# Forget-gate attention: probabilities in fewer SBUF slots, value products of two query tiles in one round, gated outputs fetched a round before their split

## The chip, the cores and the metric

The kernel is one program on one core of a Trainium2 chip. The metric is the device time of one execution in microseconds. A profiled execution gives, beside its time, the span from the first to the last instruction and a record of every engine. PE is the matrix engine (TensorE), PEld its weight loads, ACT is ScalarE, DVE is VectorE, POOL is GpSimd, and SP is SyncE, which issues most of the DMA transfers. The granted clock is the share of full speed at which PE was allowed to run.

## The reference, cut to what matters

The program is a stack of three blocks (latent attention with a sliding window, forget-gate attention, then an mLSTM mixer, cross attention and a mixture of experts). The change lies in the second, `fox_layer`, with 1024 tokens, 16 heads of width 64, and query blocks of 128:

```python
def causal_block_attention(q, k, v, log_cum=None):
    ...
        s = jnp.einsum('bqhd,bkhd->bhqk', qi, k, preferred_element_type=jnp.float32) * scale
        if lc_t is not None:
            ci = lax.dynamic_slice_in_dim(lc_t, start, QBLOCK, axis=2)
            s = s + ci[..., :, None] - lc_t[..., None, :]
        ...
        s = jnp.where(mask, s, -jnp.inf)
        p = jax.nn.softmax(s, axis=-1)
        return jnp.einsum('bhqk,bkhd->bqhd', p.astype(v.dtype), v)

def fox_layer(x, g_in, w_in, b_f, w_out):
    ...
    o = causal_block_attention(...)
    return x + (o.reshape(B, S, FOX_WIDTH) * jax.nn.silu(gate)) @ w_out
```

## The kernel before, in words

The function `fox` works through 64 steps n = 8p + i: p is one of 8 pairs of heads (a = 0 and 1 are the two heads of a pair), i is one of 8 query tiles of 128 rows. Each step goes through four stages.

- `score(n)`: PE multiplies queries and keys, three products of split numbers for each head; each head uses 64 of the 128 rows of the array. Rows of keys reach up to the query tile, so the width is 128(i+1). The results lie in PSUM banks `ps` (three) and `pd` (two). Then POOL adds the mask to the forget terms (`dm`), and DVE adds the forget terms and takes the row maximum into the tile `P` (L1259).
- `soft(n)`: ACT takes the exponential in place and sums it (L1267), DVE takes the reciprocal (`rinv`), POOL multiplies `P` by it (L1270).
- `turn(n)`: PE transposes `P` block by block into PSUM banks `pt` (two, up to four blocks in each), and ACT copies each bank into the tile `PT` (L1286). The copies of steps n = 2z and n = 2z + 1 lie side by side in one `PT`, 256 columns wide.
- `outs(n)`: PE multiplies the values by `PT` (L1301), with 64 columns of the array for each head, into the bank `po`. Of the pair z, the even step does the first half of the key blocks and the odd step the second half. Every order row of this product is two records in the trace. After i = 3 and i = 7, DVE multiplies by the gate (`go`, L1309) and ACT issues the DMA that stores `go` in the DRAM tensor `god`.

The rounds t = -2 to 65 are written out in one loop: `outs(t-2)`, `score(t+2)`, then `turn(t+1)` woven with fill work, then `soft(t+2)`. The fill is the projection of queries, keys and gates of the next pair of heads (and, for some, of values), L342 to L344, for t below 54: eight pieces for each pair of heads, six in the last. From t = 54 to 57 there is no fill. From t = 58 (p = 7) the fill is the key and value projection of the later cross attention (L1895, input `s<-x_wkv`, output `kvo`, stored in `kvd`), with as many units in each round as `FOX_FILL` says, and `ahead(t-56)`, which prepares the output projection of this layer by the table `FOX_AHEAD`: ('w', j) fetches and splits j pieces of `o_wo`, ('g', j) loads the pieces j of `god` (two halves of the tokens) into `gor` and splits each into `fh` (ACT, L348) and `fl` (DVE, L349). Then `out_proj` multiplies them (L342 to L344 again).

Order: on PE and SP the written order of the loop stands. ACT, DVE and POOL are ordered by a scheduler when the program is built; once built, every engine runs its list from the top to the bottom, so an instruction that waits holds all that stand behind it on its engine. SP's list is one queue of DMA issues: a load that waits for room holds the loads behind it.

Memory: `k.slot` gives one of 41 slots of 128 x 1024 numbers; `P`, `PT`, `V`, `x_wkv` and the split pieces live there. `k.xslot` gives one of three buffers; in this stage they hold the forget terms `lcb` of two heads (L1181, two DMAs for each pair of heads) and `gor`.

Of the kernel before, what the change touches and what calls it, by code (L numbers as in the profile page):

```python
# [58 lines left out]
LAM = 0  # L59
OUT_TILES = 4  # L60
FOX_FILL = {58: 1, 59: 2, 60: 1, 61: 2, 62: 1, 63: 1}
FOX_AHEAD = {2: (('w', 1),), 3: (('w', 1),), 4: (('g', 0),), 5: (('g', 1),), 6: (('w', 2), ('g', 2)), 7: (('w', 2),), 8: (('w', 2),), 11: (('g', 3),)}
MLA_W = (4, 0, 0.5, 1, 31)
MLA_U = 0
SW_AT = (1, 2, 3)
# [402 lines left out]
def weave(gens):  # L468
    gens = [g for g in gens if g is not None]
    while gens:  # L470
        for g in list(gens):
            try:
                next(g)
            except StopIteration:
                gens.remove(g)
# [639 lines left out]
def fox(k, ft, resid, after_tile):  # L1115
    nc, A = k.nc, k.A
# [6 lines left out]
    for i in range(NT):  # L1123
        ps = k.psd()
        for kt in range(8):
            wt, j = wv[kt // 3], kt % 3
# [15 lines left out]
    for b in range(2):  # L1142
        ps = k.pst()
        for t in range(4):
            i = b * 4 + t
            nc.tensor.matmul(ps[:16, t * 128:(t + 1) * 128], ab[:, i * 16:(i + 1) * 16], k.triu, start=True, stop=True)
        for t in range(4):
            i = b * 4 + t
            dst = nlc[:, i * 128:(i + 1) * 128]
# [9 lines left out]
    god = k.dram([8, 128, 1024], "god")  # L1159
    P, PT, po, M, WV = {}, {}, {}, {}, {}  # L1160
# [69 lines left out]
    def val(p, a, j):  # L1230
        c = p % 2 * 128 + a * 64
        return V[p // 2][j // 4][:, j % 4, c:c + 64]

    def score(n):

        p, i = divmod(n, 8)
        w = (i + 1) * 128
        qh, ql, kh, kl = qk[p]
        ps = {}
        for c in range(0, w, 512):  # L1240
            m = min(512, w - c)
            for a in range(2):
                ps[c, a] = k.psd() if c and a else k.pss()
            for l, r in ((qh, kh), (qh, kl), (ql, kh)):
                for a in range(2):
                    h = slice(a * 64, a * 64 + 64)
                    nc.tensor.matmul(ps[c, a][:, :m], l[h, i * 128:w], r[h, c:c + m], start=l is qh and r is kh, stop=l is ql)  # L1247
        for a in range(2):
            P[n, a] = k.slot([128, 1024], name="P")
            dm = k.small([128, 128], "dm", bufs=3)  # L1250
            nc.gpsimd.tensor_add(dm, lcb[p][a][:, i * 128:w], k.mask)  # L1251
            M[n, a] = 1e30
            for c in range(0, w, 512):
                m = min(512, w - c)
                for c0, c1, b in ((c, min(c + m, w - 128), lcb[p][a]), (w - 128, c + m, dm)):
                    if c1 <= c0:
                        continue
                    mx = k.small([128, 1], "m", bufs=12)
                    nc.vector.tensor_tensor_reduce(P[n, a][:, c0:c1], ps[c, a][:, c0 - c:c1 - c], b if b is dm else b[:, c0:c1],  # L1259
                                                   -1.0, M[n, a], OP.add, OP.min, mx)  # L1260
                    M[n, a] = mx

    def soft(n):
        w = (n % 8 + 1) * 128
        for a in range(2):
# [3 lines left out]
            nc.vector.reciprocal(ri, sm)  # L1269
            nc.gpsimd.tensor_scalar(sb[:, :w], sb[:, :w], ri, 0.0, op0=OP.mult, op1=OP.add)  # L1270

    def turn(n):
        i, z = n % 8, n // 2
        for a in range(2):
            p = P.pop((n, a))
            for c in range(0, i + 1, 4):
                m, q = min(4, i + 1 - c), (z, a, c // 4)
                if q not in PT:
                    PT[q] = k.slot([128, 4, 256], name="PT")
                pt = k.pst()  # L1280
                for j in range(m):
                    st["T"] = nc.tensor.transpose(pt[:, j * 128:(j + 1) * 128], p[:, (c + j) * 128:(c + j + 1) * 128], k.ident)  # L1282
                dst = PT[q][:, :m, n % 2 * 128:(n % 2 + 1) * 128]
                src = pt[:, :m * 128].rearrange("p (j n) -> p j n", j=m)
                if (a + c // 4) % 4 < 3:
                    nc.scalar.copy(dst, src)  # L1286
                else:
                    nc.vector.tensor_copy(dst, src)
                yield

    def outs(n):
        p, i = divmod(n, 8)
        if i % 4 == 0:
            po[0] = k.pso()
        o, half = po[0], i // 2 + 1
        last = half * 2 - 1
        for j in range(i % 2 * half, (i % 2 + 1) * half):
            n0 = 128 if j == last else 0
            cols = slice((last - 1) % 4 * 128 + n0, (last % 4 + 1) * 128)
            for a in range(2):  # L1300
                nc.tensor.matmul(o[a * 64:(a + 1) * 64, cols], val(p, a, j), PT[n // 2, a, j // 4][:, j % 4, n0:],  # L1301
                                 start=j == 0, stop=j == last)
            if j % 4 == 3 or j == last:
                for a in range(2):
                    PT.pop((n // 2, a, j // 4))
        if i % 4 == 3:
            t = k.slot([128, 512], name="go")
            cols = slice(i // 4 * 512, (i // 4 + 1) * 512)
            nc.vector.scalar_tensor_tensor(t, o, 0.5, gt[p][:, cols], op0=OP.mult, op1=OP.mult)  # L1309
            k.q.dma_start(out=god[p, :, cols], in_=t)  # L1310
# [5 lines left out]
    def fill(t):  # L1316

        p, i = divmod(t, 8)
        if t < 0:
            return [units[-1][t + 6]()]  # L1320
        if p >= 7:
            return k.mem.fill(FOX_FILL, t) + [ahead(t - 56)]
        if i == 0:
            u, g = prep(p + 1), p // 2 + 1
            if p < 6:
                u += [L(v_unit, g, x + p % 2 * 2) for x in range(2)]
                if p % 2 == 0:
                    u[2], u[4] = L(v_weights, u[2], g, 0), L(v_weights, u[4], g, 1)
            units[p] = u
        return [units[p][i]()] if i < len(units[p]) else []  # L1330

    go, W = FT(k), []

    def ahead(i):

        yield
        for what, j in FOX_AHEAD.get(i, ()):
            if what == "w":
                for _ in range(j):
                    W.append(k.w_get(k.fo[len(W)], 0))  # L1340
                    yield
            else:
                for hf in range(2):
                    t = k.xslot([128, 2, 512], name="gor")
                    nc.sync.dma_start(out=t, in_=god[2 * j:2 * j + 2, :, hf * 512:(hf + 1) * 512].rearrange("k p n -> p k n"))
                    hi, lo = go.piece(hf, j)
                    k.split(hi, lo, t)
                    yield

    a, b, c = FOX_SKEW  # L1350
    with k.tc.manual_schedule(engines=FOX_MAN):
        for t in range(-a, 64 - c):
            if 0 <= t + c:
                outs(t + c)
            if t + a < 64:
                score(t + a)
            weave(([turn(t + b)] if 0 <= t + b < 64 else []) + (fill(t) if t < 64 else [ahead(t - 56)]))
            if t + a < 64:
                soft(t + a)
# [788 lines left out]
class Moe:  # L2148
# [212 lines left out]
    def place(self, part, i0, row, col, iota, lo, hi, acc, t, B, ch, ps):  # L2361


        k, V, TT, w = self.k, self.k.nc.vector, self.k.nc.vector.tensor_tensor, hi - lo
        per = lambda v, n: v.unsqueeze(2).to_broadcast([128, 4, n])
        if part == 0:
            gg = self.gates[:, i0 * 2:i0 * 2 + 4]
            ident = t[:, 1016:1020]
            tok = self.tok[:, i0:i0 + 2].unsqueeze(2).to_broadcast([128, 2, 2])
            TT(ident.rearrange("p (n j) -> p n j", j=2), tok, row.rearrange("p (n j) -> p n j", j=2), op=OP.subtract)  # L2370
            rh = B["rh"] = k.slot([128, 4, 128], name="rh")
            ch = B["ch"] = ch().rearrange("p (n a w) -> p n a w", n=4, a=2)
            TT(rh, self.iota.unsqueeze(1).to_broadcast([128, 4, 128]), per(row, 128), op=OP.is_equal)
            TT(ch[:, :, 0, :], iota[:, lo:hi].unsqueeze(1).to_broadcast([128, 4, w]), per(col, w), op=OP.is_equal)
            V.tensor_mul(ch[:, :, 1, :], ch[:, :, 0, :], per(gg, w))
            V.tensor_mul(ch[:, :, 0, :], ch[:, :, 0, :], per(ident, w))
        elif part == 1:
            B["pl"] = ps()
            for n in range(4):
                k.nc.tensor.matmul(B["pl"][:, 0:2 * w], B["rh"][:, n, :], B["ch"][:, n, :, :].rearrange("p a b -> p (a b)"),  # L2380
                                   start=n == 0, stop=n == 3)
        else:
            acc = acc.rearrange("p (a b) -> p a b", a=2)[:, :, lo:hi]
            V.tensor_add(acc, acc, B["pl"][:, 0:2 * w].rearrange("p (a b) -> p a b", a=2))
            B.clear()
# [546 lines left out]
```

## Time and profile before

| what | us |
|---|---|
| median of 3 runs | 2276.36 (2274.25 to 2277.02) |
| the profiled execution | 2273.73 |
| its span | 2272.0 |
| PE busy in the span | 2177.8 |

The profiled execution is 2.63 us below the median, and 1.73 us of it lie outside the span. The rows that the prediction uses stand further down. In rows of a timeline, the first number is the start, the second how long the record or the merged records lasted, xN how many were merged; a bracket at the end tells how long the engine sat idle before it, and what released it. Records of matmuls overlap (they are pipelined), so the pace is read from the start of one to the start of the next.

### The profile page before, as it was taken

What the parts mean: (1) busy time and instruction counts of PE and PEld (TensorE: products, weight loads), DVE (VectorE), ACT (ScalarE), POOL (GpSimd) and SP (SyncE); (2) the same over time, 40 slices, a digit from 0 to 9 for tenths busy, and PEclk for the clock granted to TensorE, in tenths of its full rate; (3) what the DMA queues carried; (4) which work ended last, traced back from release to release, by engine and by line L of the source; (5) the groups of instructions that cost most, each with busy time, mean ns of one, the idle gap of its engine ahead of it and who ended that gap; (6) DMA issues with size and microseconds to landing.
All of it is one profiled execution on the core that took longest, in us unless ns stands there. A gap on an engine that the chain in (4) does not pass through costs nothing. (4 is left out here: it accounts for less than half of the span.)

```text
span 2272.0 us, 33492 instructions
## 1 busy us (share of the span) xinstructions
PE 2177.8 (96%) x12596; PEld 1742.1 (77%) x12596; DVE 1153.4 (51%) x2848; ACT 946.5 (42%) x1986; POOL 452.9 (20%) x620
## 2 busy tenths in 40 slices
PE   7999999999999999999999999999999999899797
PEld 7888868888877778777778799887677888667564
DVE  6322677844244343433443322688355547756544
ACT  5322667823254444544542222355103122556454
POOL 2000455410122222222300000121010112222121
PEclk9999999999999999999999999999999999999899
DMA  4112221133121111211352221426575125779674
GB/s 167 38 47 97 87 59 39 59 126 115 57 70 47 34 58 51 75 38 43 119 178 102 98 80 48 135 70 232 194 277 225 67 93 213 254 231 295 218 217 167
DMA packets 91396, 273.70 MB, mean 120 GB/s; under 512 B 10956, under 2 KB 24012, under 8 KB 91232
## 3 DMA queue, kind: packets, MB, share of 16 engines
q1 hardware_dynamic: 75616, 225.32, 28.6%
q0 software_dynamic: 6624, 24.12, 4.5%
q10 hardware_dynamic: 8992, 22.09, 2.6%
q8 instruction: 100, 1.64, 0.3%
q14 instruction: 64, 0.52, 0.1%
HBM read 202.73 MB, written 65.62 MB: 118 GB/s over the span
## 5 line engine op out<-in xcount | busy, mean ns | idle before, releaser
L342 PE MATMUL pd<-fh,wh 128*128 128x512 f32 x784 | 323.0, 412 | 3.3 <-DVE qk L1169 3.0
L344 PE MATMUL pd<-fh,wl 128*128 128x512 f32 x784 | 309.0, 394 | 0.5 <-DVE wl L320 0.5
L343 PE MATMUL pd<-fl,wh 128*128 128x512 f32 x784 | 308.4, 393 | 0.0
L342 PE MATMUL pd<-wh,fh 128*128 128x256 f32 (+3 forms) x808 | 259.8, 322 | 2.6 <-DVE n L1429 2.5
L344 PE MATMUL pd<-wh,fl 128*128 128x256 f32 (+3 forms) x808 | 255.1, 316 | 0.0
L343 PE MATMUL pd<-wl,fh 128*128 128x256 f32 (+3 forms) x808 | 254.5, 315 | 0.0
L320 DVE TENSOR_TENSOR wl<-w,wh 128x1024 fp32r<-128x1024 f32 (+5 forms) x92 | 108.2, 1181 | 151.0 <-ACT wh L318 150.0
L344 PEld LDWEIGHTS pd<-fh,wl 128*128 128x128 f32 x784 | 147.3, 188 | 35.3 <-DVE wl L320 1.0
L342 PEld LDWEIGHTS pd<-fh,wh 128*128 128x128 f32 x784 | 147.5, 188 | 34.2 <-DVE qk L1169 4.7
L343 PEld LDWEIGHTS pd<-fl,wh 128*128 128x128 f32 x784 | 148.0, 189 | 27.2
L342 PEld LDWEIGHTS pd<-wh,fh 128*128 128x128 f32 x808 | 152.7, 189 | 14.4 <-DVE n L1429 3.2
L343 PEld LDWEIGHTS pd<-wl,fh 128*128 128x128 f32 x808 | 152.7, 189 | 10.9 <-issue 1.0
L344 PEld LDWEIGHTS pd<-wh,fl 128*128 128x128 f32 x808 | 152.4, 189 | 10.1 <-issue 0.2
L1286 ACT COPY PT<-pt 128x512 f32<-128x512 f32 (+2 forms) x192 | 90.9, 477 | 154.0 <-PE pt L1282 144.0
L318 ACT CAST wh<-w 128x1024 fp32r<-128x1024 f32 (+5 forms) x99 | 97.3, 989 | 127.8 <-PE pd L343 97.8
L1251 POOL TENSOR_TENSOR dm<-lcb,mask 128x128 f32<-128x128 f32 x128 | 60.0, 474 | 409.6 <-DVE m L1259 283.7
L1259 DVE CUSTOM_DVE_ANT_0 P<-ps,lcb 128x512 f32<-128x512 f32 (+3 forms) x112 | 64.1, 572 | 95.8 <-PE ps L1247 94.4
L1267 ACT ACTIVATE P<-P,m 128x256 f32<-128x256 f32 (+7 forms) x128 | 99.4, 777 | 23.1 <-DVE m L1259 20.4
L1282 PE MATMUL pt<-ident,P 128*128 128x128 f32 x576 | 97.3, 280 | 7.2 <-ACT PT L1286 5.9
L1270 POOL TENSOR_SCALAR P<-P,rinv 128x256 f32<-128x256 f32 (+7 forms) x128 | 98.1, 770 | 27.0 <-issue 12.5
L2413 DVE TENSOR_TENSOR ml<-mw,mh 128x1024 fp32r<-128x1024 f32 x66 | 80.1, 1226 | 30.8 <-DMA mw<-w_moe 15.7
L1282 PEld LDWEIGHTS pt<-ident,P 128*128 128x128 f32 x576 | 68.1, 141 | 32.8 <-issue 15.5
(515 smaller groups left out, 4688.5 us busy)
## 6 DMA issues: line engine op xcount, KB each, us to landing
mw<-w_moe SPq DMA_DIRECT2D x70, 512.0 KB, 7.5
w<-w_moe SPq DMA_DIRECT2D x26, 512.0 KB, 5.5
w<-o_wc SPq DMA_DIRECT2D x24, 512.0 KB, 3.8
xr<-xs SPq DMA_DIRECT2D x18, 512.0 KB, 4.6
s<-x_wkv SPq DMA_DIRECT2D x16, 512.0 KB, 6.0
lcb<-dn SPq DMA_DIRECT2D x16, 512.0 KB, 4.6
wkd<-kvw SPq DMA_DIRECT2D x32, 256.0 KB, 3.1
kw<-wkd SPq DMA_DIRECT2D x16, 512.0 KB, 7.4
```

Source lines behind the costliest of these rows:

```text
L318: nc.scalar.copy(hi[:, :n], raw[:, :n])
L320: (eng or nc.vector).tensor_sub(lo[:, :n], raw[:, :n], hi[:, :n].bitcast(F32))
L342: first = mm(out, lhs[0], rhs[0], start=start, stop=False)
L343: mm(out, lhs[0], rhs[1], start=False, stop=False)
L344: mm(out, lhs[1], rhs[0], start=False, stop=stop)
L1251: nc.gpsimd.tensor_add(dm, lcb[p][a][:, i * 128:w], k.mask)
L1259: nc.vector.tensor_tensor_reduce(P[n, a][:, c0:c1], ps[c, a][:, c0 - c:c1 - c], b if b is dm else b[:, c0:c1], -1.0, M[n, a], OP.add, OP.m ...
L1267: nc.scalar.activation(sb[:, :w], sb[:, :w], AF.Exp, bias=M.pop((n, a)), scale=-1.0, accum_out=sm)
L1270: nc.gpsimd.tensor_scalar(sb[:, :w], sb[:, :w], ri, 0.0, op0=OP.mult, op1=OP.add)
L1282: st["T"] = nc.tensor.transpose(pt[:, j * 128:(j + 1) * 128], p[:, (c + j) * 128:(c + j + 1) * 128], k.ident)
L1286: nc.scalar.copy(dst, src)
L2413: nc.vector.tensor_sub(W[c][1], raw[c], W[c][0].bitcast(F32))
```

## The change

- In `score`, for i below 4 both heads' `P` lie in one slot of 1024 columns, half each; before, each head had its own slot. For i of 4 and above nothing changes.
- `PT` is given out by a new function `place`, which packs the blocks of both heads into slots of four blocks: one slot in place of two for i = 0 and 1, two for i = 2 and 3, three in place of four for i = 4 and 5, four for i = 6 and 7.
- In the loop, `outs` is called in rounds of odd t alone, for the even step and then for the odd one. The products are the same.
- In `ahead`, loading `gor` is a step of its own ('l'), one round ahead of the split ('g') that reads it; `gor` lies in a slot, no longer in one of the three `x` buffers; the two halves of piece 3 are loaded and split apart from each other (the first half in rounds 63 and 64, the second after the loop).

```diff
--- before.py
+++ after.py
@@ -59,7 +59,8 @@
 LAM = 0
 OUT_TILES = 4
 FOX_FILL = {58: 1, 59: 2, 60: 1, 61: 2, 62: 1, 63: 1}
-FOX_AHEAD = {2: (('w', 1),), 3: (('w', 1),), 4: (('g', 0),), 5: (('g', 1),), 6: (('w', 2), ('g', 2)), 7: (('w', 2),), 8: (('w', 2),), 11: (('g', 3),)}
+FOX_AHEAD = {2: (('w', 1),), 3: (('w', 1), ('l', 0, 0, 1)), 4: (('g', 0, 0, 1), ('l', 1, 0, 1)), 5: (('g', 1, 0, 1), ('l', 2, 0, 1)), 6: (('w', 2), ('g', 2, 0, 1)),
+             7: (('w', 2), ('l', 3, 0)), 8: (('w', 2), ('g', 3, 0)), 10: (('l', 3, 1),), 11: (('g', 3, 1),)}
 MLA_W = (4, 0, 0.5, 1, 31)
 MLA_U = 0
 SW_AT = (1, 2, 3)
@@ -1245,8 +1246,9 @@
                 for a in range(2):
                     h = slice(a * 64, a * 64 + 64)
                     nc.tensor.matmul(ps[c, a][:, :m], l[h, i * 128:w], r[h, c:c + m], start=l is qh and r is kh, stop=l is ql)
+        t = k.slot([128, 1024], name="P") if i < 4 else None
         for a in range(2):
-            P[n, a] = k.slot([128, 1024], name="P")
+            P[n, a] = t[:, a * 512:(a + 1) * 512] if i < 4 else k.slot([128, 1024], name="P")
             dm = k.small([128, 128], "dm", bufs=3)
             nc.gpsimd.tensor_add(dm, lcb[p][a][:, i * 128:w], k.mask)
             M[n, a] = 1e30
@@ -1269,18 +1271,25 @@
             nc.vector.reciprocal(ri, sm)
             nc.gpsimd.tensor_scalar(sb[:, :w], sb[:, :w], ri, 0.0, op0=OP.mult, op1=OP.add)
 
+    def place(z, a, j):
+
+        half = z % 4 * 2 + 2
+        x = a * half + ((j + half - 4 if j < 4 else j - 4) if a and half > 4 else j)
+        if (z, x // 4) not in PT:
+            PT[z, x // 4] = k.slot([128, 4, 256], name="PT")
+        return PT[z, x // 4], x % 4
+
     def turn(n):
         i, z = n % 8, n // 2
         for a in range(2):
             p = P.pop((n, a))
             for c in range(0, i + 1, 4):
-                m, q = min(4, i + 1 - c), (z, a, c // 4)
-                if q not in PT:
-                    PT[q] = k.slot([128, 4, 256], name="PT")
+                m = min(4, i + 1 - c)
                 pt = k.pst()
                 for j in range(m):
                     st["T"] = nc.tensor.transpose(pt[:, j * 128:(j + 1) * 128], p[:, (c + j) * 128:(c + j + 1) * 128], k.ident)
-                dst = PT[q][:, :m, n % 2 * 128:(n % 2 + 1) * 128]
+                t, x = place(z, a, c)
+                dst = t[:, x:x + m, n % 2 * 128:(n % 2 + 1) * 128]
                 src = pt[:, :m * 128].rearrange("p (j n) -> p j n", j=m)
                 if (a + c // 4) % 4 < 3:
                     nc.scalar.copy(dst, src)
@@ -1298,11 +1307,8 @@
             n0 = 128 if j == last else 0
             cols = slice((last - 1) % 4 * 128 + n0, (last % 4 + 1) * 128)
             for a in range(2):
-                nc.tensor.matmul(o[a * 64:(a + 1) * 64, cols], val(p, a, j), PT[n // 2, a, j // 4][:, j % 4, n0:],
-                                 start=j == 0, stop=j == last)
-            if j % 4 == 3 or j == last:
-                for a in range(2):
-                    PT.pop((n // 2, a, j // 4))
+                t, x = place(n // 2, a, j)
+                nc.tensor.matmul(o[a * 64:(a + 1) * 64, cols], val(p, a, j), t[:, x, n0:], start=j == 0, stop=j == last)
         if i % 4 == 3:
             t = k.slot([128, 512], name="go")
             cols = slice(i // 4 * 512, (i // 4 + 1) * 512)
@@ -1329,28 +1335,31 @@
             units[p] = u
         return [units[p][i]()] if i < len(units[p]) else []
 
-    go, W = FT(k), []
+    go, W, raw = FT(k), [], {}
 
     def ahead(i):
 
         yield
-        for what, j in FOX_AHEAD.get(i, ()):
+        for what, j, *h in FOX_AHEAD.get(i, ()):
             if what == "w":
                 for _ in range(j):
                     W.append(k.w_get(k.fo[len(W)], 0))
                     yield
+            elif what == "l":
+                for hf in h:
+                    raw[hf, j] = k.slot([128, 2, 512], name="gor")
+                    nc.sync.dma_start(out=raw[hf, j], in_=god[2 * j:2 * j + 2, :, hf * 512:(hf + 1) * 512].rearrange("k p n -> p k n"))
             else:
-                for hf in range(2):
-                    t = k.xslot([128, 2, 512], name="gor")
-                    nc.sync.dma_start(out=t, in_=god[2 * j:2 * j + 2, :, hf * 512:(hf + 1) * 512].rearrange("k p n -> p k n"))
+                for hf in h:
                     hi, lo = go.piece(hf, j)
-                    k.split(hi, lo, t)
+                    k.split(hi, lo, raw.pop((hf, j)))
                     yield
 
     a, b, c = FOX_SKEW
     with k.tc.manual_schedule(engines=FOX_MAN):
         for t in range(-a, 64 - c):
-            if 0 <= t + c:
+            if 0 <= t + c and t % 2:
+                outs(t + c - 1)
                 outs(t + c)
             if t + a < 64:
                 score(t + a)
```

How the instructions stand. PE, with `po` the value product, `ps` a score, `pt` a transpose, `pd` with `s` the cross-attention fill (rows of scores left out). Before, rounds 58 and 59:

```order
L1282 MATMUL pt_11577<-ident,P_11512 128x128 x3
L1301 MATMUL po_11592<-PT_11471,V_9883 64x256
L1301 MATMUL po_11592<-PT_11475,V_9883 64x256
L1247 MATMUL ps_11595<-qk_10901,qk_10899 128x512
...
L1282 MATMUL pt_11631<-ident,P_11563 128x128 x4
L1895 MATMUL pd_11645<-s_11637,s_11641 128x256 x4
L1895 MATMUL pd_11645<-s_11639,s_11641 128x256 x4
L1301 MATMUL po_11592<-PT_11471,V_9883 64x128
L1301 MATMUL po_11592<-PT_11475,V_9883 64x128
L1247 MATMUL ps_11675<-qk_10901,qk_10899 128x512
```

Now:

```order
L1290 MATMUL pt_11529<-ident,P_11452 128x128 x3
L1248 MATMUL ps_11545<-qk_10853,qk_10851 128x512
...
L1290 MATMUL pt_11581<-ident,P_11510 128x128 x4
L1904 MATMUL pd_11595<-s_11587,s_11591 128x256 x4
L1904 MATMUL pd_11595<-s_11589,s_11591 128x256 x4
L1311 MATMUL po_11623<-PT_11429,V_9845 64x256 x2
L1311 MATMUL po_11623<-PT_11429,V_9845 64x128 x2
L1248 MATMUL ps_11628<-qk_10853,qk_10851 128x512
```

The product of step 56 (64x256) has left the place ahead of the score in round 58 and stands in round 59, right ahead of that of step 57 (64x128).

ACT, rounds 60 and 61: `PT` copies, exponentials (ACTIVATE), the casts of `gor`, and the store of `go`. Before:

```order
L1286 COPY PT_11716<-pt_11819 128x2x128
L1267 ACTIVATE P_11795,sum_11859<-P_11795,m_11802 128x896
L1286 COPY PT_11733<-pt_11836 128x4x128
L1267 ACTIVATE P_11804,sum_11864<-P_11804,m_11811 128x896
L348 CAST fh_11832<-gor_11830 128x1024
L1286 COPY PT_11747<-pt_11855 128x2x128
L1903 COPY kvo_11846<-pd_11825 128x256
L1907 DMA kvd<-kvo_11846 128x256
L348 CAST fh_11851<-gor_11849 128x1024
L1310 DMA god<-go_11873 128x512
L1286 COPY PT_11910<-pt_11911 128x4x128
L1286 COPY PT_11917<-pt_11918 128x3x128
```

Now:

```order
L1295 COPY PT_11667<-pt_11765 128x4x128
L349 CAST fh_11782<-gor_11700 128x1024
L1295 COPY PT_11671<-pt_11771 128x2x128
L1269 ACTIVATE P_11747,sum_11811<-P_11747,m_11754 128x896
L1295 COPY PT_11691<-pt_11786 128x4x128
L1269 ACTIVATE P_11756,sum_11816<-P_11756,m_11763 128x896
L1912 COPY kvo_11796<-pd_11777 128x256
L349 CAST fh_11799<-gor_11702 128x1024
L1295 COPY PT_11671<-pt_11803 128x2x128
L1916 DMA kvd<-kvo_11796 128x256
L1316 DMA god<-go_11829 128x512
L1295 COPY PT_11871<-pt_11866 128x4x128
```

The casts of piece 0 stand earlier among the work of round 60 (behind the first copy, and behind the second exponential), and they read loads that are issued in round 59.

SP, rounds 58 to 61. Before:

```order
L282 DMA w_11654<-o_wo 128x1024
L246 DMA s_11720<-x_wkv 128x1024
L282 DMA w_11731<-o_wo 128x1024
L246 DMA s_11751<-x_wkv 128x1024
L246 DMA s_11823<-x_wkv 128x1024
L1345 DMA gor_11830<-god 128x2x512
L1345 DMA gor_11849<-god 128x2x512
L246 DMA s_11923<-x_wkv 128x1024
L1345 DMA gor_11930<-god 128x2x512
L1345 DMA gor_11950<-god 128x2x512
L246 DMA s_11962<-x_wkv 128x1024
```

Now:

```order
L283 DMA w_11604<-o_wo 128x1024
L247 DMA s_11673<-x_wkv 128x1024
L283 DMA w_11684<-o_wo 128x1024
L1351 DMA gor_11700<-god 128x2x512
L1351 DMA gor_11702<-god 128x2x512
L247 DMA s_11707<-x_wkv 128x1024
L247 DMA s_11775<-x_wkv 128x1024
L1351 DMA gor_11807<-god 128x2x512
L1351 DMA gor_11809<-god 128x2x512
L247 DMA s_11879<-x_wkv 128x1024
L247 DMA s_11914<-x_wkv 128x1024
```

The two loads of piece 0 have moved ahead of two loads of `x_wkv`, and those of piece 1 ahead of one.

## Rows read from the trace of the kernel before

**Rows 1.** The page's first part: busy time and share of each engine.

```profile
PE 2177.8 (96%) x12596; PEld 1742.1 (77%) x12596; DVE 1153.4 (51%) x2848; ACT 946.5 (42%) x1986; POOL 452.9 (20%) x620
```

**Rows 2.** Stretches: start:end, us, PE busy (records), granted clock, DMA share, GB/s.

```profile
600.00:1100.00 500.00, 496.98 (x3163) 1.00 0.16 55
...
1142.00:1148.50 6.50, 1.21 (x6) 1.00 0.50 161
1148.50:1152.40 3.90, 3.84 (x12) 0.56 0.82 257
```

**Rows 3.** PE's timeline: a round without, two with a value product.

```profile
606.16 0.40 PE L344 MATMUL pd<-fh,wl 128*128 128x512 f32 x1
606.49 0.55 PE L1247 MATMUL ps<-qk,qk 64*128 64x128 f32 x6
...
793.65 0.39 PE L344 MATMUL pd<-fh,wl 128*128 128x512 f32 x1
793.97 1.08 PE L1301 MATMUL po<-PT,V 128*64 128x256 f32 x8
794.98 1.14 PE L1247 MATMUL ps<-qk,qk 64*128 64x512 f32 x7
...
830.48 1.95 PE L1301 MATMUL po<-PT,V 128*64 128x256 f32 x16
832.36 0.79 PE L1247 MATMUL ps<-qk,qk 64*128 64x384 f32 x6
```

**Rows 4.** Timelines of DVE, PE and POOL about the last step of a pair.

```profile
741.34 2.21 POOL L1270 TENSOR_SCALAR P<-P,rinv 128x1024 f32<-128x1024 f32 x2
743.45 0.66 PE L1282 MATMUL pt<-ident,P 128*128 128x128 f32 x4
...
805.26 1.23 DVE L320 TENSOR_TENSOR wl<-w,wh 128x1024 fp32r<-128x1024 f32 x1 [0.31 <-PE ps L1247]
807.00 0.68 DVE L1259 CUSTOM_DVE_ANT_0 P<-ps,lcb 128x512 f32<-128x512 f32 x1
...
813.10 1.52 PE L1301 MATMUL po<-PT,V 128*64 128x256 f32 x12
815.03 0.66 PE L1282 MATMUL pt<-ident,P 128*128 128x128 f32 x4
...
813.41 3.19 POOL L1270 TENSOR_SCALAR P<-P,rinv 128x1024 f32<-128x1024 f32 x2
...
814.06 1.54 DVE L320 TENSOR_TENSOR wl<-w,wh 128x1024 fp32r<-128x1024 f32 x1 [1.78 <-ACT wh L318]
```

**Rows 5.** PE's timeline in rounds 56 and 58, which have little or no fill.

```profile
1108.32 0.80 PE L1247 MATMUL ps<-qk,qk 64*128 64x384 f32 x6
1109.05 0.66 PE L1282 MATMUL pt<-ident,P 128*128 128x128 f32 x4
...
1115.96 0.65 PE L1282 MATMUL pt<-ident,P 128*128 128x128 f32 x4 [0.56 <-POOL P L1270]
```

**Rows 6.** Timelines of PE, ACT and SP in rounds 60 to 62.

```profile
1148.56 1.09 PE L1282 MATMUL pt<-ident,P 128*128 128x128 f32 x4 [5.35 <-ACT PT L1286]
1149.43 3.14 PE L1895 MATMUL pd<-s,s 128*128 128x256 f32 x8
...
1156.28 1.08 PE L1301 MATMUL po<-PT,V 128*64 128x256 f32 x8
...
1144.53 1.04 ACT L348 CAST fh<-gor 128x1024 fp32r<-128x1024 f32 x1 [5.16 <-DMA gor<-god]
...
1128.17 12.56 SPq L1345 DMA_DIRECT2D gor<-god  x2
```

**Rows 7.** SP's and PE's timelines in rounds 59 and 60; DMA issues: KB, us to landing.

```profile
1127.26 0.86 SPq L246 DMA_DIRECT2D s<-x_wkv  x2
...
1133.90 0.81 PE L1895 MATMUL pd<-s,s 128*128 128x256 f32 x3
...
s<-x_wkv SPq DMA_DIRECT2D x8, 512.0 KB, 6.3
```

## The prediction, made before the changed kernel ran

> **What bounds the kernel now.** I read the page's first part first: PE is busy for 2177.8 of 2272.0 us [rows 1]. An average says little about one stage, so the next view is the table by stretches. From 600 to 1100 us, rounds below 54 or so of the forget-gate attention, PE is busy for 496.98 of 500 us at full clock [rows 2]: there a wait of another engine costs nothing, and only PE's own time counts, or a new wait of PE. [...]
>
> **Part 1: fewer separate value products.** [...] The even steps 0 to 60 are 31 products that now run straight into the odd one; step 62 stood next to 63 already. [...] So 31 x 0.155 = 4.8 us less, all on PE, where nothing hides it. [...]
>
> [...]
>
> **Part 2: the cover that goes.** The product of an even step also gave POOL time: in that round PE came to the transposes of the step before that much later. The critical case is the last step of each pair of heads, transposed in a round that loses a product of 12 records, 1.45 us. For head pair 2, PE began the product at 813.10 and the transposes at 815.03, while POOL normalised that step's two `P` from 813.41 on for 3.19 us together [rows 4]. The first was ready just as PE came, and 1.45 us earlier it would not be. POOL's start hangs on a DMA for the forget terms, which waits for DVE to read the old ones; DVE began that at 807.00, held up by a weight split from 805.26 and a `go` behind it [rows 4]. That split hangs on the round before, which itself now ends about 1.0 us earlier, as it has lost its product too. So POOL's start moves forward by up to 1.0 us for head pairs 0, 2 and 4. For pair 1 POOL began at 741.34 and had the first tile some 1.1 us later, while PE came at 743.45 [rows 4]: 1 us to spare, and POOL moves by some 0.4. Pairs 3 and 5 look like pair 1, with more to spare. I estimate 0.1 to 0.3 us of waiting in each of four pairs, 0.6 us in all. If nothing moves forward, it is up to 1.45 in each of three and 0.45 in one, 4.8. If POOL moves as far as PE, 0.
>
> [...]
>
> **Part 3: the last head pair, rounds 54 to 59.** Without fill the chain score, softmax, transpose is bare. In round 56 PE went from a product of sixteen records (1.88 us, [rows 3]) into the score at 1108.32 and the transposes at 1109.05 [rows 5]. Without the product PE comes there some 1.9 us early. The score must wait a little for a bank, and the transposes wait for POOL: about 1.0 us lost. The product then stands in round 57 and delays the score of step 59 by some 1.4 us. On that chain PE was already waiting, 0.56 us ahead of 1115.96 [rows 5]. So the transposes, and the fill behind them, come 0.8 to 0.9 us later. Sum 1.8 us; bounds 0.5 (the second chain catches up) and 3.5 (both products' whole length).
>
> **Part 4: gated outputs fetched a round ahead.** The hole first. ACT stood 5.16 us until a `gor` load had landed and cast it from 1144.53; behind it in ACT's list stood the store of `go` and the `PT` copies. The two `gor` issues stretch over 12.56 us on SP's queue, because the second waited for one of the three `x` buffers. PE, which needs a copied `pt` bank, idled 5.35 us, and eight records of the cross-attention fill then took 3.14 us at the low clock [rows 6]. Of the 3.84 us of work at clock 0.56 [rows 2], 3.84 x 0.44 = 1.7 us are the clock. Hole 5.35 + 1.7 = 7.1 us. With the loads in slots, issued in round 59 and 60 for casts in 60 and 61, that wait goes. What is late next? DVE gets one split ahead of its reciprocals (1.2 us) and another ahead of `go`. The maximum of step 63 then starts about 2.4 us behind PE's score, and ACT's copies follow a `go` store that comes about 0.5 us later than the transposes; but PE has 7 us of fill in that round, and both `pt` banks come free before the fill between them is done. So I take the whole 7.1; bounds 7.1 and 3 (half of it comes back as another link of the same chain). Copies, splits and loads keep their number and size; packing `P` and `PT` changes no instruction's length, only which slots are free. The exponential of the second head waits for nothing on POOL, although both lie in one tile.
>
> The new queue order costs something: two loads of `gor` pass two of `x_wkv`, whose issue was at 1127.26 [rows 7]. At some 0.45 us an issue they go 0.9 us later, to 1128.15, and land 6.3 us later [rows 7], at 1134.5. The fill that reads the first began at 1133.90 [rows 7] and would now begin near 1134.2. 0.3 us; bounds 0 and 2 (the four loads share the bandwidth).
>
> **Sum.** -4.8 + 0.6 + 1.8 - 7.1 + 0.3 = -9.2 us. The profiled execution, 2273.73, becomes 2264.5; it lies 2.63 under the median, so the median of 2276.36 becomes **2267.1 us**. What comes behind should keep the gain: it works in the same order as before, and its loads are let go by PE's and DVE's progress, so they move with it.
>
> **Rivals.** (a) *The hole only changes its owner.* The chain go, store, copies, maximum, exponential of step 63 still stops PE, with the clock drop. Against it: the load's 5.16 us was the one long wait on ACT. Then part 4 gives 7.1 - 5 = 2.1, sum -4.2, median 2272.2. (b) *The cover was worth what it hid.* POOL doesn't move forward, 4.8 us, and the last pair costs 3.5: sum -4.8 + 4.8 + 3.5 - 7.1 + 0.3 = -3.3, median 2273.1. For it: the spare time of almost nothing for pair 2 [rows 4]. (c) *Slower: SP's queue blocks.* The first `gor` now needs a slot. If that slot comes free as late as the `x` buffer did (12.56 us on the queue [rows 6]), the `x_wkv` loads behind it go 12.6 us later, land near 1146.5, and PE, which needs the first at 1134.2, waits 12 us and falls to the low clock (1.7): -9.2 + 12 + 1.7 = +4.5, median 2280.9. It decides from a hold of about 9 us; the rows show no slot wait of that length. (d) *The product's 0.155 us is not saved*, because the order alone moves it elsewhere: sum -4.4, median 2272.0.
>
> **How the numbers follow.** Chances: the forecast 0.77, (a) 0.08, (b) 0.07, (c) 0.04, (d) 0.04. Within 0.2% (4.55 us) is about what a measurement can tell from no change. (a), (b) and (d) fall there, 0.19, and 0.02 of the forecast's 0.77: same 0.21, faster 0.75, slower 0.04. The best that the bounds allow is -4.9 + 0 + 0.5 - 7.1 + 0 = -11.5 (2264.9); the other end is where (a), (b) and (d) lie, 2272.0 to 2273.1. The runs shown spread by 2 us below and 1 us above their median, so the range is 2263.0 to 2273.5.
>
> **What would show it.** PE's records of L1301 stand in 32 groups and no longer in 63. Right for part 1: each two rounds below 50 take 0.15 us less. Part 2: a wait of PE on POOL once in a pair of heads, some tenths. Part 3: a new wait of 1 us ahead of the transposes in round 56, and a longer one in round 58. Part 4: no idle time of PE over 2 us and no clock under 1.0 between 1100 and 1200 us, and out_proj begins some 9 us earlier. Wrong would be a wait of SP on a slot ahead of `gor`, an idle stretch on PE with ACT or DMA as releaser in rounds 60 to 63, or waits on POOL of a microsecond in every pair.

## The result: slower, and where the time came from

The changed kernel took 2298.45 us in the median (2296.30 to 2300.91, 4 runs) beside 2276.69 for the kernel before: a ratio of 1.0095, 95% interval 1.0081 to 1.0109. The forecast was 2267.1 us, and slower had a chance of 4 in 100. The profiled execution of after took 2300.91 us with a span of 2299.1, 27.1 more than the span before. PE and its weight loads are busy for longer, the other engines within 3 us of [rows 1]:

```profile
PE 2189.1 (95%) x12596; PEld 1755.2 (76%) x12596; DVE 1153.1 (50%) x2848; ACT 944.6 (41%) x1986; POOL 455.8 (20%) x620
```

PE has as many records as before, so the 11 us more of busy time are records that took longer, and the rest of the 27 is idle time of PE.

Starts on PE's timeline of the two kernels tell where the lateness arises:

| PE starts | before | after | later by |
|---|---|---|---|
| score of step 0 | 606.49 | 606.46 | 0.0 |
| score of step 56, in round 54 | 1100.79 | 1123.26 | 22.5 |
| first cross-attention fill, round 58 (L1895, now L1904) | 1117.44 | 1144.33 | 26.9 |
| score of step 63 | 1138.91 | 1172.90 | 34.0 |
| out_proj, first record | 1171.36 | 1197.85 | 26.5 |
| last output sum (L2762, now L2771) | 2260.96 | 2287.76 | 26.8 |

So 22.5 of the 27 us arise in rounds below 54, where PE had no long wait before, 11.5 more at the end of the stage, and 7.5 come back when the old hole is gone. What stands behind keeps the lateness as it is. (At the score of round 54 after still has the product of step 52 to do, 1.4 us, and at the first fill that of step 56, 0.6 us; from the score of step 63 on the same work is done in both.)

The table by stretches of after, the same view as [rows 2] (start:end, us, PE busy (records), granted clock, DMA share, GB/s), gives the first sign: 480.11 us busy of 500 in place of 496.98, and a clock of 0.98 in place of 1.00. Two of its stretches of 20 us, each with a wait of 1.6 us, show 0.91 and 1.00:

```profile
600.00:1100.00 500.00, 480.11 (x3023) 0.98 0.15 51
...
780.00:800.00 20.00, 18.38 (x98) 0.91 0.12 32
860.00:880.00 20.00, 18.37 (x113) 1.00 0.08 26
...
1100.00:1200.00 100.00, 94.74 (x569) 0.93 0.41 139
```

Next PE's waits from 600 to 1200 us (line waited for, us in total, times, longest). Of before:

```profile
PE pt L1282 <- ACT PT L1286: 5.9, 2, 5.3
PE pd L342 <- DVE qk L1169: 3.0, 7, 0.5
PE pt L1282 <- POOL P L1270: 1.2, 3, 0.6
```

Of after, the four largest:

```profile
PE pd L343 <- DVE qk L1170: 11.4, 7, 1.7
PE pd L343 <- DVE qk L1176: 8.3, 6, 1.4
PE pd L1904 <- DMA s<-x_wkv: 2.6, 1, 2.6
PE pt L1290 <- POOL P L1272: 1.4, 2, 0.9
```

The wait for ACT's `PT` copy, 5.3 us of it the old hole, is gone, as forecast. In its place stand 13 waits of PE for VectorE's `qk`, 19.7 us together where 3.0 stood (two in each of the seven head pairs that have the projections as fill, in the last of them one), and one for an `x_wkv` load. `qk` is the evacuation of a projection: PE needs the PSUM bank `pd` again, and VectorE is the last to read it.

One such wait close up. PE's timeline, after (start, duration; the bracket is the idle time ahead and who ended it): the last record of a projection unit, the score of step 4, transposes, then the next unit:

```profile
632.95 0.39 PE L345 MATMUL pd<-fh,wl 128*128 128x512 f32 x1
633.27 0.97 PE L1248 MATMUL ps<-qk,qk 64*128 64x512 f32 x6
...
634.45 0.66 PE L1290 MATMUL pt<-ident,P 128*128 128x128 f32 x4
636.77 0.50 PE L343 MATMUL pd<-fh,wh 128*128 128x512 f32 x1 [1.66 <-DVE qk L1170]
...
637.95 0.63 PE L344 MATMUL pd<-fl,wh 128*128 128x512 f32 x1
```

VectorE beside it, after:

```profile
634.27 1.23 DVE L321 TENSOR_TENSOR wl<-w,wh 128x1024 fp32r<-128x1024 f32 x1 [3.41 <-PE ps L1248]
635.42 0.68 DVE L1261 CUSTOM_DVE_ANT_0 P<-ps,lcb 128x512 f32<-128x512 f32 x1
636.03 0.08 DVE L1261 DVE_READ_ACCUMULATOR2_ANT m<- 128x1 f32 x1
636.03 0.69 DVE L1170 SCALAR_TENSOR_TENSOR qk<-pd,qk 128x512 fp32r<-128x512 f32 x1
```

and of before, VectorE's weight split, evacuation and maximum, then PE's transposes and next unit:

```profile
634.28 1.23 DVE L320 TENSOR_TENSOR wl<-w,wh 128x1024 fp32r<-128x1024 f32 x1 [3.40 <-ACT wh L318]
635.43 0.68 DVE L1169 SCALAR_TENSOR_TENSOR qk<-pd,qk 128x512 fp32r<-128x512 f32 x1
636.03 0.68 DVE L1259 CUSTOM_DVE_ANT_0 P<-ps,lcb 128x512 f32<-128x512 f32 x1
```

```profile
635.03 0.66 PE L1282 MATMUL pt<-ident,P 128*128 128x128 f32 x4
636.17 0.50 PE L342 MATMUL pd<-fh,wh 128*128 128x512 f32 x1 [0.48 <-DVE qk L1169]
```

Two things have moved, and both count. PE starts its transposes at 634.45 and no longer at 635.03, 0.58 us earlier, as the value product (four records) is not there; the bank is not empty earlier for that. And the scheduler, which orders VectorE's list, now has the first maximum ahead of the evacuation, so the bank is free 0.60 us later (636.03 and not 635.43 for its start). 0.58 + 0.60 is the 1.18 by which the wait grew, from 0.48 to 1.66. There are two `pd` banks; the score of a step with more than four tiles takes the other one, so the next unit needs the one being emptied. In step 6 of six pairs the same happens with a wait of 1.4 us where there was none. In both kernels a weight split of 1.2 us stands on VectorE ahead of the two; what an evacuation ahead of that split would give was not run.

Soon after the wait the projection records take 0.63 us in place of 0.39: the granted clock is 0.50 from 638 to 641 us and 1.00 again from 642. Such a fall is the 0.91 of the stretch 780 to 800 (0.09 x 20 = 1.8 us). It comes behind the wait in step 4, not behind the one in step 6: in that third pair the waits, 1.62 and 1.36 us, end at 787.71 and 807.79, and the table in stretches of 4 us has

```profile
784.00:788.00 4.00, 2.38 (x19) 0.98 0.13 23
788.00:792.00 4.00, 4.00 (x14) 0.60 0.31 111
...
804.00:808.00 4.00, 2.64 (x19) 1.00 0.09 19
808.00:812.00 4.00, 4.00 (x21) 1.00 0.62 243
```

So it is in each of the six pairs in which the clock fell: it is 0.50 for over 3 us, and that begins within 1 us of the end of a wait of 1.6 us.

The sum for rounds below 54: waits 19.7 - 3.0 = +16.7; 26 merged products at an estimated 0.155, -4.0 (between the 0.14 of [rows 3] and the 0.17 of e5_early_only, both worked out under Part 1 below); the product of step 52, not yet done, -1.4. So 22.5 - 16.7 + 4.0 + 1.4 = 11.2 us are left for the clock (10.8 to 11.6 with 0.14 to 0.17). In stretches of 20 us eight of 25 have a clock under 1.00, and what they lack adds to 0.54 of a stretch, 10.8 us: six falls of 1.8.

### The profile page after: what moved, and what is told of

It reads as the page before. It is cut to its first block, busy times and chain, and to the rows that moved or that the text cites. A ratio compares the mean times of both kernels' runs of the same rounds, so it can differ in the third digit from the quotient of the medians.

```text
span 2299.1 us, 33445 instructions
## 1 busy us (share of the span) xinstructions
PE 2189.1 (95%) x12596; PEld 1755.2 (76%) x12596; DVE 1153.1 (50%) x2848; ACT 944.6 (41%) x1986; POOL 455.8 (20%) x620
## 5 line engine op out<-in xcount | busy, mean ns | idle before, releaser
L344 PEld LDWEIGHTS pd<-wl,fh 128*128 128x128 f32 x808 | 152.5, 189 | 10.8 <-issue 1.0
L1253 POOL TENSOR_TENSOR dm<-lcb,mask 128x128 f32<-128x128 f32 x128 | 65.8, 519 | 435.1 <-DVE m L1261 301.6
```

Of the source, the lines that this page charges most:

```text
L344: mm(out, lhs[0], rhs[1], start=False, stop=False)
```

## The experiments

Theory, *uncovered bank*: between the end of a projection unit and the next need of its bank, the value product was the work that kept PE busy while ACT and VectorE emptied the bank. Rivals: *packing* (fewer, shared slots make the waits), *order alone* (the scheduler's place for the evacuation is all of it), and *any round without a product waits*. L numbers of a kernel made from one of the two differ from those above by at most three. Each ratio is to runs of the kernel before that were taken beside it; their medians lie between 2275.7 and 2277.1 us.

| run | median us | ratio to before, 95% interval | waits for qk, 600 to 1100 us | clock there |
|---|---|---|---|---|
| after | 2298.45 | 1.0081 to 1.0109 | 19.7 | 0.98 |
| e1_separate | 2268.89 | 0.9961 to 0.9980 | 3.0 | 1.00 |
| e2_dve_first | 2281.81 | 1.0014 to 1.0034 | 11.7 | 1.00 |
| e4_merge_only | 2298.91 | 1.0081 to 1.0117 | 19.7 | 0.98 |
| e5_early_only | 2268.92 | 0.9955 to 0.9980 | 1.5 | 1.00 |
| e10_max_first | 2284.27 | 1.0024 to 1.0053 | 9.9 | 1.00 |
| e7_two_turns | 2287.22 | 1.0026 to 1.0051 | 15.2 | 1.00 |
| e9_last_separate | 2293.70 | 1.0057 to 1.0091 | 19.7 | 0.99 |
| e3_early | 2265.64 | 0.9932 to 0.9965 | 1.4 | 1.00 |
| e8_early_late_gor | 2261.86 | 0.9915 to 0.9948 | 1.5 | 1.00 |

**Which part of the change.** e1_separate is the changed kernel with the products back in each round:

```diff
-            if 0 <= t + c and t % 2:
-                outs(t + c - 1)
+            if 0 <= t + c:
                 outs(t + c)
```

> The changed kernel with the value products back in every round; packing and early reload stay. Theory (uncovered bank): between the end of a projection unit and the next unit PE had the product as work while ACT and DVE emptied the unit's pd bank; in even rounds that work is gone. With the products back, PE's waits for qk between 600 and 1100 us fall from 19.7 to about 3.0 us, the clock stays at 1.00 there, and the last score of the stage comes at 1140 to 1146 us in place of 1174. What stays is the early reload: 7.1 us less for the old hole, and 0.3 to 5.6 more for the x_wkv loads: 2270 to 2275 us. Rival (packing): the waits come from fewer, shared slots: they stay, and the time is 2290 or more.

e4_merge_only is the opposite, those three lines of the change put into the kernel before.

> The kernel before with the value products of two steps in every odd round, and nothing else: no packing, no early reload. Theory (uncovered bank): the two waits a head pair are there as in the changed kernel (about 17 us more than before), with one clock drop a pair (about 11), less 0.5 a pair, and 4 us in the last head pair; the old hole of 7 us stays: last score near 1168 to 1174 us, time 2300 to 2308 us. Rival (packing): no waits, about 4.8 us less than before, 2272.

Waits of PE in e1_separate, then in e4_merge_only, 600 to 1200 us (those for `qk`, `x_wkv` and the old hole):

```profile
PE pd L343 <- DVE qk L1170: 3.0, 7, 0.5
PE pd L1903 <- DMA s<-x_wkv: 1.3, 2, 0.8
```

```profile
PE pd L342 <- DVE qk L1169: 11.4, 7, 1.7
PE pd L342 <- DVE qk L1175: 8.3, 6, 1.4
PE pt L1282 <- ACT PT L1286: 5.0, 2, 4.4
```

The merging alone makes the waits, to the tenth, and with it alone the kernel is as slow as the changed one (2298.9, a little under the 2300 expected). Packing and early reload make none, and without the merging they are worth 2275.7 - 2268.9 = 6.8 us (the 2268.9 lies just under the 2270 to 2275 expected). The rival of packing falls.

**Product or order.** e2_dve_first keeps the merging and tells the scheduler that the evacuation goes ahead of the step's first maximum (cut; `ev` is the last evacuation given to VectorE):

```diff
+                    r = nc.vector.tensor_tensor_reduce(P[n, a][:, c0:c1], ...)
+                    ev = st.pop("ev", None)
+                    k.order(r, ev if i > 3 else None)
```

> The changed kernel, and for steps of 5 tiles and more (4 to 7 of a head pair) VectorE is told to empty the pd bank (qk, gt) before the first maximum of the step's scores, as it stood in the kernel before. Theory (uncovered bank): the order is half of it, one maximum of 0.60 us: the 13 waits go from 1.62 and 1.38 to about 1.03 and 0.78 us, 7.7 us less; if the clock no longer falls, up to 11 more: 2280 to 2291 us. Rival (the order is all of it): the waits return to 0.45 us once a pair, full clock, about 2276 to 2280 us. Rival (packing): no change, 2298.

e10_max_first does the reverse in the kernel before, `k.order(ev if i in (4, 6) else None, r)`.

> The kernel before with one thing changed: in steps 4 and 6 of a head pair VectorE empties the pd bank behind the first maximum of the step's scores, as it does in the changed kernel; the value products stay in every round. It is the fourth corner of product (there, gone) and order (bank first, maximum first). Theory (uncovered bank, the two prices add up): the wait in step 4 grows from 0.43 by a maximum of 0.60 to 1.03 us, and in step 6, where PE came 0.14 us after the bank was free, 0.46 us of waiting appear; 7 x 0.60 + 6 x 0.46 = 7.0 us more, no lower clock, as waits of 1.03 and 0.78 had none: 2281 to 2285 us. Rival (the order costs only where the product is gone): the waits stay at 0.43 and 0, 2276 us. Rival (the order alone brings the clock down): 2290 us or more.

Waits of PE in e2_dve_first, then in e10_max_first:

```profile
PE pd L343 <- DVE qk L1170: 7.1, 7, 1.0
PE pd L343 <- DVE qk L1176: 4.6, 6, 0.8
```

```profile
PE pd L342 <- DVE qk L1169: 7.3, 7, 1.1
PE pd L342 <- DVE qk L1175: 2.6, 7, 0.4
```

With these two the square is full: waits of 3.0 us with product and old order, 9.9 with the order alone, 11.7 with the product gone alone, 19.7 with both. The two prices nearly add up (3.0 + 6.9 + 8.7 = 18.6), and both were needed. The lower clock shows in the last corner only: with waits of 1.0 and 0.8 us a pair, or 1.1 and 0.4, the clock stays at 1.00; with 1.6 and 1.4 it falls in most pairs. So e2 won 16.6 us (15.7 when both are taken against their own runs of before) where its waits are only 8.0 us shorter. "Order alone" falls, and so does "the order costs only where the product is gone".

**Is it PE's arrival?** e7_two_turns keeps merging and VectorE's order, and pulls the second group of transposes ahead of the first piece of the projection unit; no work is added:

```diff
+            tr = [turn(t + b)] if 0 <= t + b < 64 else []
+            if t < 56 and (t + a) % 8 in (4, 6) and t + a < 64:
+                next(tr[0])
-            weave(([turn(t + b)] if 0 <= t + b < 64 else []) + (fill(t) if t < 64 else [ahead(t - 56)]))
+            weave(tr + (fill(t) if t < 64 else [ahead(t - 56)]))
```

> The changed kernel, and in the rounds of the two waits a head pair the second group of transposes goes ahead of the first piece of the projection unit; no work is added or taken, and VectorE's order stays. Theory (uncovered bank): any work of PE covers the bank: the wait for qk is 0.45 us shorter in step 4 (four transposes, 1.62 to 1.17) and 0.25 in step 6 (two transposes, 1.38 to 1.1), 4.7 us in all; if waits of that size no longer cost clock, as in e2_dve_first, 11 us more: 2283 to 2294 us. Rival (the loss belongs to the missing product or to the order on VectorE, and is not PE's arrival): no change, 2298.

```profile
634.30 1.09 PE L1290 MATMUL pt<-ident,P 128*128 128x128 f32 x8
636.61 0.50 PE L343 MATMUL pd<-fh,wh 128*128 128x512 f32 x1 [1.22 <-DVE qk L1170]
```

PE's timeline shows eight transposes ahead of the unit and 1.22 us of wait in place of 1.66. So transposes cover the bank as the product did. 4.5 us less waiting brought 11.2 us, as the clock stays up.

**The same merging in the other rounds.** e5_early_only is the kernel before with both products in the even round; the odd step's product needs nothing that the even step's doesn't, so it can go a round earlier:

```diff
-            if 0 <= t + c:
-                outs(t + c)
+            if 0 <= t + c and t % 2 == 0:
+                outs(t + c)
+                outs(t + c + 1)
```

> The kernel before with both value products of a pair of steps in the even round, so that the odd step's product goes a round earlier and the odd rounds have none. Theory (uncovered bank): the price hangs on the bank that is empty late. In odd rounds of the kernel before, the bank was free 0.7 us (step 5) and 1.4 us (step 7) before PE came for it, and they lose 0.37 and 0.8 us of product: no wait; the wait of 0.43 us in step 4 goes too, since the even rounds have more work. 31 x 0.155 = 4.8 and 7 x 0.43 = 3.0 us less: about 2269 us, 2266 to 2272. Rival (any round without a product waits): two waits of over a microsecond a pair and clock drops again, 2295 us or more.

PE's waits for `qk` in e5_early_only, and its row of the table by stretches:

```profile
PE pd L342 <- DVE qk L1169: 1.5, 7, 0.3
```

```profile
600.00:1100.00 500.00, 497.83 (x3205) 1.00 0.17 58
```

The odd rounds, bare now, have no wait. From pair to pair (from the score of step 16 to that of step 24) a pair takes 813.94 - 743.24 = 70.70 us, where it took 814.55 - 742.97 = 71.58. So it matters in which rounds the work goes missing, and "any round without a product waits" falls.

**The last head pair.** e9_last_separate is the changed kernel with separate products from round 56 on.

> The changed kernel with the value products separate from round 56 on alone (the last head pair and what follows). Theory: of the 22.5 us by which the changed kernel is late at the score of round 54, nothing changes; from there to the first fill it took 21.1 us, and e1_separate 16.2: 4.9 us less, and with it the wait for x_wkv (2.6 and some 3 of clock) falls to 1.3: 2288 to 2294 us. Rival (the loss of the last head pair comes from packing or reload): no change, 2298.

From the score of round 54 to the first fill it took 1135.97 - 1118.49 = 17.5 us, where after took 21.1; with the products counted alike (1.4 us of step 52 taken off both, 0.6 of step 56 put onto after) 16.1 and 20.3, and e1_separate took 16.2. So these 4 us are the merging's. The time moved by 4.8, within the expectation, but not for the reason given: the score of round 54 came 4.8 us earlier than in after with the same waits, since fewer stretches of this execution had the low clock, and PE still waited 2.2 us for `x_wkv` where 1.3 was expected (on SP's queue it was 2.17 us from the first of the two `gor` issues to that load's, 1151.20 to 1153.37, and 0.99 in e1_separate). How much of the median's 4.8 is the last pair stays open.

**Queue order.** e3_early is e5's loop in the changed kernel, packing and reload included. e8_early_late_gor is e3_early with two more `yield` ahead of the 'l' step, so that one more `x_wkv` load goes ahead of the first pair of `gor` loads.

> The changed kernel (packing and early reload stay) with both value products of a pair of steps in the even round, as in e5_early_only. Theory (uncovered bank): the gains of the two parts stand side by side, as they lie in different rounds: e1_separate had 6.8 us from the early reload, e5_early_only 6.8 from the merging: 2275.7 - 13.6 = 2262 us, 2259 to 2265; no wait for qk over 0.3 us, clock 1.00 from 600 to 1100, no idle of PE over 3 us in the last head pair. Rival (the gains overlap): what the merging gained is taken back where PE then comes to the x_wkv loads earlier: 2266 to 2269 us.

> As e3_early, with the first pair of early gor loads behind one more x_wkv load on SP's queue. Theory (queue order): the wait of PE for x_wkv (2.6 us in the changed kernel, 1.3 in e1_separate) comes from the two gor loads ahead of it; it falls under 0.5 us, 1 to 2.5 us less than e3_early. Rival (bandwidth): the loads share the transfers, and the order changes nothing: within 0.5 us of e3_early, with the wait still there.

PE's timeline in e3_early, then in e8_early_late_gor, after the transposes of round 60:

```profile
1129.27 0.87 PE L1290 MATMUL pt<-ident,P 128*128 128x128 f32 x6
1132.04 1.96 PE L1904 MATMUL pd<-s,s 128*128 128x256 f32 x8 [1.90 <-DVE m L1261]
```

```profile
1129.42 0.87 PE L1290 MATMUL pt<-ident,P 128*128 128x128 f32 x6
1130.13 1.89 PE L1906 MATMUL pd<-s,s 128*128 128x256 f32 x8
```

The profile puts the 1.90 us down to VectorE's maximum. But in e8_early_late_gor the same maximum ends later still, on VectorE's timeline,

```profile
1132.01 0.08 DVE L1261 DVE_READ_ACCUMULATOR2_ANT m<- 128x1 f32 x1
```

and PE began at 1130.13, so it was not the maximum. The edit between the two moves SP's issues alone, so it was the `x_wkv` load. The order of two kinds of load on one queue was worth these 1.9 us; the medians differ by 3.8, more than the 1 to 2.5 expected, with runs of each kernel 3 to 6 us apart. e3_early lies 0.6 us above its 2259 to 2265 and just under its rival's 2266 to 2269: part of the gains does overlap, by a wait for `x_wkv` as that rival says. e8_early_late_gor beats both kernels: 2261.86 us, 0.5 to 0.9% under before.

## Why the prediction was wrong, step by step

| term | forecast | measured |
|---|---|---|
| merged products (part 1) | -4.8 | -4.3 to -5.3 |
| cover that goes, POOL (part 2) | +0.6 | 0 |
| cover that goes, the bank `pd`: waits | not in the sum | +16.7 |
| the clock behind these waits | not in the sum | +11.2 |
| last head pair (part 3) | +1.8 | +3.6 |
| the hole (part 4) | -7.1 | -7.5 |
| `x_wkv` behind `gor` (part 4) | +0.3 | +5.9 |
| sum | -9.2 | +25 (out_proj is 26.5 later) |

Of the 1.5 us that the sum lacks, some 1.1 are the clock of 0.72 from 1144 to 1148 us, at the first cross-attention fill, which is in no row of this table.

- *What bounds the kernel.* That below round 54 "only PE's own time counts, or a new wait of PE" was right, and then the new waits were looked for in one place only.
- *Part 1* was right. A pair of steps 16 to 24 in e5_early_only is 0.88 us shorter; 0.2 of it is the shorter wait (0.43 to 0.2), the rest is 0.17 for each of four products, against 0.155. No run shows the 0.155 itself, nor the 4.9 at the lower end of the range: [rows 3] give 1.01 us for eight records and 1.88 for sixteen, so 0.87 for eight more and 1.01 - 0.87 = 0.14 beside the records of a product, and e5_early_only gives 0.17; for 31 products that is 4.3 to 5.3 us.
- *Part 2 is the step that failed.* It asked what the even step's product covers, and listed POOL alone. In after no wait for POOL stands below round 54 (its 1.4 us lie in the last head pair); e4_merge_only has two there, 0.27 and 0.21 us, of the size foreseen. The bank `pd`, which ACT and VectorE empty in the same stretch, was not on the list, although PE was already waiting 0.4 to 0.5 us for it in each pair: a cover with nothing to spare. Nor was VectorE's list looked at, which the scheduler makes afresh when PE's order changes. Behind the waits the clock came down (0.98 from 600 to 1100 us in place of 1.00), and no term had a clock in it but the hole.
- *POOL in [rows 4].* Neither of its two pairs of normalisations ran without a weight split on VectorE beside it. The 3.19 us has the split of 1.54 (814.06); beside the 2.21, on VectorE's timeline of before, ran

```profile
742.48 2.14 DVE L320 TENSOR_TENSOR wl<-w,wh 128x1024 fp32r<-128x1024 f32 x1 [2.85 <-ACT wh L318]
```

2.14 us, where with POOL idle one took 1.23 (805.26). So the splits took longer beside POOL's work; what they cost POOL, 2.21 and 3.19 don't show.
- *Part 3* was too small: 4.4 us later in this stretch, with the products counted alike 4.4 - 1.4 + 0.6 = 3.6, just outside the bounds of 0.5 to 3.5. From 1132 to 1136 us the clock was 0.57 and from 1140 to 1144 it was 0.85, 1.7 + 0.6 us. Without the clock 1.3 are left, which the bounds held.
- *Part 4*, the hole, was right: no wait for a cast of `gor`, and from the score of step 63 to out_proj 24.95 us in place of 32.45. The new queue order was mis-sized. In after, PE's timeline,

```profile
1160.43 0.87 PE L1290 MATMUL pt<-ident,P 128*128 128x128 f32 x6
1163.92 3.75 PE L1904 MATMUL pd<-s,s 128*128 128x256 f32 x8 [2.61 <-DMA s<-x_wkv]
```

SP's queue,

```profile
1155.53 0.90 SPq L1351 DMA_DIRECT2D gor<-god  x2
1156.52 1.13 SPq L247 DMA_DIRECT2D s<-x_wkv  x2
```

and the table by stretches:

```profile
1160.00:1164.00 4.00, 1.39 (x13) 0.91 1.05 409
1164.00:1168.00 4.00, 4.00 (x11) 0.50 1.05 411
```

The `x_wkv` loads went out 1.0 us later, as forecast. But counted from the score of round 59 PE came for them 1.0 us earlier (11.53 us after it, with the fill 0.71 us behind the transposes as before, and not 12.54), as round 60 had lost its product too. And PE could start on the first only 7.4 us after its issue, where 6.3 was the median landing, with the DMA share at 1.05. From 1160.43 to the fill went 3.49 us where before it was 0.71 (1133.19 to the 1133.90 of [rows 7]), 2.8 more, and the work behind it took 3.1 us more at the low clock (0.50 from 1164 to 1168 us, 0.74 from 1168 to 1172). With the product in its place 0.8 us of this wait were left in e1_separate, but 2.2 in e9_last_separate; with the queue's order put right as well (e8_early_late_gor) none.

- *What comes behind should keep the gain*: it kept the loss, 26.5 us at out_proj and 26.8 at the last sum.
- *The rivals.* (b), the cover was worth what it hid, was the right idea on the wrong resource, priced at 4.8 us. (c), a load that waits for a slot, did not happen: the `x_wkv` load that PE waited for was issued behind the `gor` loads at once. So slower, with its chance of 4 in 100, came true by another way than the one it was given for. Of the signs of being wrong that the prediction named, one came, PE idle in round 60 with a DMA as releaser, 2.6 us; for the larger loss, waits of a microsecond on a bank, it had named none.

## What to carry to other kernels

Before work is taken from between two uses of a PSUM bank, list every bank and buffer that is emptied in that stretch, and for each the spare time between free and needed; a wait of a few tenths in the trace of before (here 0.4 to 0.5 us) says that it has none. Look also at what a scheduler does with the other engines' lists, since one instruction that changed places there cost as much here (0.60 us) as the work that was moved (0.58). Where work may go to one of two rounds, take it from the round whose banks come free early (here the odd rounds: PE waited 1.5 us for `qk` in e5_early_only, 19.7 in e4_merge_only).

## What the runs showed of the hardware

The clock's price did not grow with the waits: a fall came or didn't. Below round 54 each fall stands right behind a wait of 1.6 us in step 4, none behind the 1.4 in step 6, and costs some 1.8 us, as much as the wait again. With the same waits the clock fell in six of seven head pairs in after (not from 860 to 880 us, behind a wait of 1.63), in five in e4_merge_only and in three in e9_last_separate, which reached round 54 4.8 us earlier than after. Why it fell behind one of these waits and not behind another stays open. Waits of 1.2 and 1.15, of 1.0 and 0.8, or of 1.1 and 0.4 us brought it down in none of these pairs of e7_two_turns, e2_dve_first and e10_max_first. The length of one wait is not all of it: in the last head pair of after the clock fell (0.57 from 1132 to 1136 us) behind waits of 0.25 and 0.85. Whether executions of one kernel differ by which pairs fall is not shown, as each kernel has one trace.
